# Time mixing's chunk recurrence: heads in pairs on diagonal corners of the array

## The chip, the core and the metric

One core of a Trainium2 chip. Its engines run side by side, each with its own list of instructions: TensorE (PE in the profile, its weight loads PEld) multiplies matrices into PSUM, VectorE (DVE) and ScalarE (ACT) work element by element, GpSimd (POOL) does a few small operations, and SyncE (SP) issues most transfers. The metric is the device time of one execution in microseconds; lower is better.

## The reference

A decoder block over 2048 tokens of 1024 channels. After a norm and one large projection, half of the mixing is RWKV-7 time mixing with 8 heads of 64 channels, half is differential attention with 4 heads; then an output projection and a gated MLP with a short convolution follow. The change lies in the time mixing, whose core is a recurrence over tokens with a 64 x 64 state per head:

```python
def step(state, inp):
    r_t, w_t, k_t, v_t, kk_t, a_t = inp
    sa = einsum('bhvk,bhk->bhv', state, -kk_t)
    state = (state * w_t[:, :, None, :]
             + sa[..., None] * (kk_t * a_t)[:, :, None, :]
             + v_t[..., None] * k_t[:, :, None, :])
    return state, einsum('bhvk,bhk->bhv', state, r_t)
```

All inputs and products of this part are float32.

## The kernel before

**Stages.** The input is projected in two halves of 1024 tokens (class `Proj`, tile `pp`, lines L99 to L101: each product is made of three, of high and low parts). The time mixing (class `Rwkv`) runs in 16 groups of 128 tokens; its stages are emitted in turns, a few after each block of the projection, later a few after each unit of the attention (class `Attn`: scores in a tile that is also called `sp`, L775 to L780; transposed weights `tp`, `at`; output `op`, L819). The output projection and the MLP come after both. Within an engine the order of instructions is fixed beforehand by a scheduler that goes through the program with modelled times; so products of the time mixing stand between projection matmuls or attention's, which fill TensorE while the recurrence waits for other engines.

**A group** is two chunks of 64 tokens (`NC` = 2). `prepare(g)` loads its rows, makes the decayed operands `AR` (64 columns against which the state is read for the recurrence, 64 for the output) and `BK` (b and k), the score products `se`, `so` of even and odd heads (L470), masks them into `M` (L474), sends the diagonal blocks through DRAM (`adr`, L478, then `ab`), transposes v into the lower half of `sav` (L490), and transposes `BK` into `bkt` (L497). `invert(g)` inverts 32 x 32 blocks on VectorE (L515, L517) and puts the result back into `M` by way of DRAM (`xdr`, L520, L523; `bda`, `bdx`, `x1t`); `join(g)` fills the block off the diagonal (`xp`, L545 to L554).

**`scan(g)`** goes through the two chunks. Channels lie on partitions, two heads (an even and an odd one) to a block of 128: index `hb` is the block, `e` the head in it. The state is kept as four 128 x 128 blocks whose corners off the diagonal stay zero. Per chunk:
- `rp` (L570, L573): for each block a product of the whole state block (128 rows, 64 columns of `AR`), then for each of the two heads a product of `M`'s lower half and `sav`'s lower half (key times value), added in PSUM; `rsb` is its copy by ScalarE (L575).
- `sp` (L578): eight products of the inverse in `M`'s upper half with `rsb`, all on partitions 0 to 63; copied into `sav`'s upper half (L579).
- `up` (L583): four 128 x 128 products of `bkt` and `sav`; VectorE adds the state's corners (L588) and multiplies by the decay (L591), a half of the partitions at a time.
- `yp` (L594, L597): per block one product of the state, then two of `sav`, 64 columns each; VectorE adds it to `ybv` (L600).

The previous group's `post` (norm and gate: tiles `mp`, `vs`, `gp`) is taken in between. The PSUM tiles of `scan`, `join` and `post` share the tag `rc` with two banks, those of `prepare` the tag `ra` with two, the projection has four (`mm`).

Of the kernel before, what the change touches and what calls it, by code (L numbers as in the profile page):

```python
# [34 lines left out]
def load_table(nc, cx, pool, eng, rows, name):  # L35
    """rows: list of DRAM APs [n, 128]; the result, once called, gives an SBUF tile [128, sum n] with the rows as
    columns."""
# [17 lines left out]
def rms_rstd(nc, cx, pool, src, n, eps, name, junk):  # L55
    """[128,1] = (mean(src^2) + eps)^-0.5 over the free axis; src is a list of APs."""
# [10 lines left out]
def norm_rows(nc, cx, pool, dst, src, gain, t):  # L67
    """dst = rms-normalised rows of src times gain; both SBUF [128, 1024], tokens x channels."""
# [9 lines left out]
def transpose_split(nc, cx, ps, xn, xh, xl, t, tag, bufs):  # L78
    """xn: SBUF [128, 1024] tokens x channels; writes tokens t*128.. of xh/xl, lists of [128, 8, GRP] tiles."""
# [16 lines left out]
def mm3(nc, out, lh, ll, rh, rl, n):  # L96
    """out = sum over kb of (lh+ll)^T (rh+rl) without ll*rl; callables give the operands of kb."""
    for kb in range(n):
        nc.tensor.matmul(out, lh(kb), rh(kb), start=(kb == 0), stop=False)  # L99
        nc.tensor.matmul(out, lh(kb), rl(kb), start=False, stop=False)  # L100
        nc.tensor.matmul(out, ll(kb), rh(kb), start=False, stop=(kb == n - 1))  # L101
# [24 lines left out]
class Proj:  # L126
    """Projections of x by w_in, one half of the tokens at a time."""
# [25 lines left out]
    def load(self, t, first=None):  # L153
        """128 tokens of normalised x, transposed and split; the second half's rows come from prepare()."""
# [22 lines left out]
    def prepare(self, t):  # L177
        """Normalises 128 tokens of the second half."""
# [14 lines left out]
    def pair(self, a, b, w=None):  # L193
        """Two blocks, the first tokens of both before the last."""
# [5 lines left out]
    def start(self, first):  # L200
        """Loads the first half and does its first two blocks."""
# [20 lines left out]
    def shift(self, cb, g, pp):  # L222
        """Token shift of an RWKV block."""
# [49 lines left out]
def rwkv_consts(tc, nc, cx, I):  # L273
# [46 lines left out]
    with tc.tile_pool(name="rkd", bufs=1, side="right") as pool:  # L320
        z = pool.tile([P, 4, P], F32, name="selz")
        nc.vector.memset(z, 1.0)
        # rows h of each 32-row block: 1 where 0 <= 128*hb + ch - 64*h < 64
# [23 lines left out]
    for i in range(2):  # L347
        s = c.tile([P, 4, P], F32, name=f"state{i}")
# [5 lines left out]
def rsqrt_bcast(nc, cx, pool, bank, op, val, i, nm):  # L354
    """bank: PSUM [128, 4, RG], whose first 8 columns hold a value for each token and head; it becomes
    op(value, val)^-0.5, channels x tokens."""
# [12 lines left out]
class Rwkv:  # L369
    """Time mixing, 128 tokens at a time, in four stages per group."""  # L370
# [12 lines left out]
    def prepare(self, g):  # L383
# [71 lines left out]
        tt(BK[:, :, :, 0, :], c4(b2), c4(ip), op=ALU.mult)  # L455
        tt(BK[:, :, :, 1, :], c4(kp), c4(ip), op=ALU.mult)
# [19 lines left out]
        for d in range(2):  # L476
            ds_ = slice(32 * d, 32 * d + 32)
            nc.sync.dma_start(adr[d].rearrange("b j i -> j b i"), M[ds_, :, :, ds_].rearrange("j c h i -> j (c h) i"))  # L478
# [10 lines left out]
        for q in range(2):  # L489
            nc.scalar.copy(sav[64:128, q].rearrange("p h x -> p (h x)"),  # L490
                           vt[64 * q:64 * q + 64].rearrange("p h x -> p (h x)"))
        bkt = T([P, NC, 512], "bkt", SB)
        for c in range(NC):
# [3 lines left out]
            nc.scalar.copy(bkt[:, c, :], bt.rearrange("p h x -> p (h x)"))  # L497

        self.live[g] = dict(AR=AR, M=M, sav=sav, bkt=bkt, ybv=ybv, pc=pc, sg=sg, X=X, ab=ab)
        yield  # L500

    def invert(self, g):
# [5 lines left out]
        for q in range(4):  # L508
            qs = slice(32 * q, 32 * q + 32)
            nc.sync.dma_start(cx.bda[qs, :, qs], mq[0:32, :, q, 32:64])  # L510
# [10 lines left out]
        for d in range(2):  # L521
            ds_ = slice(32 * d, 32 * d + 32)
            nc.sync.dma_start(M[ds_, :, :, ds_].rearrange("j c h i -> j (c h) i"),  # L523
                              xdr[d].rearrange("b m s i -> (m s) b i"))
# [10 lines left out]
    def join(self, g):  # L535
        """The blocks off the diagonal of the inverse."""
# [3 lines left out]
        mv = M.rearrange("p c h x -> p (c h) x")  # L540
# [13 lines left out]
        nc.scalar.copy(mv[0:32, :, 32:64], bank[0:32].rearrange("p t (q i) -> p (t q) i", q=4))  # L554
        yield

    def scan(self, g):
        """The state over the group's chunks, with the last group's post() in between."""
# [595 lines left out]
```

## Time and profile before

| | |
|---|---|
| median of 3 runs | 3289.52 us (3286.41 to 3295.87) |
| span of the profiled execution | 3295.9 us |
| TensorE busy | 3178.5 us, 96%, 16579 matmul instructions |
| VectorE, ScalarE, GpSimd busy | 1923.8, 1167.9, 332.6 us |
| bytes moved by DMA | 282.30 MB |

The profiled execution's own time stands at the upper end of the three; nothing of it lies around its span. Busy times of TensorE come from modelled ends of overlapping matmuls, so the distance from one start to the next says more than a duration.

### The profile page before, as it was taken

What the parts mean: (1) busy time and instruction counts of PE and PEld (TensorE: products, weight loads), DVE (VectorE), ACT (ScalarE), POOL (GpSimd) and SP (SyncE); (2) the same over time, 40 slices, a digit from 0 to 9 for tenths busy, and PEclk for the clock granted to TensorE, in tenths of its full rate; (3) what the DMA queues carried; (4) which work ended last, traced back from release to release, by engine and by line L of the source; (5) the groups of instructions that cost most, each with busy time, mean ns of one, the idle gap of its engine ahead of it and who ended that gap; (6) DMA issues with size and microseconds to landing.
All of it is one profiled execution on the core that took longest, in us unless ns stands there. A gap on an engine that the chain in (4) does not pass through costs nothing.

```text
span 3295.9 us, 44432 instructions
## 1 busy us (share of the span) xinstructions
PE 3178.5 (96%) x16579; PEld 2594.6 (79%) x16579; DVE 1923.8 (58%) x4898; ACT 1167.9 (35%) x2268; POOL 332.6 (10%) x441
## 2 busy tenths in 40 slices
PE   8999999999989989898999999999999999999997
PEld 6887777777777767677888888888888788888886
DVE  5246555455457868568655455555556655555556
ACT  4233322232225555467633422222223422222223
POOL 3001000010022232233200000000000000000002
PEclk9999999999878999899999999999999999999999
DMA  5355523234372252415244311111112411111112
GB/s 159 96 158 165 146 87 99 82 82 104 91 123 59 53 104 58 72 53 136 78 141 166 122 51 52 45 45 56 48 45 82 155 52 45 45 54 49 52 33 83
DMA packets 361177, 282.30 MB, mean 86 GB/s; under 512 B 95823, under 2 KB 307378, under 8 KB 360962
## 3 DMA queue, kind: packets, MB, share of 16 engines
q1 hardware_dynamic: 333874, 247.11, 25.9%
q0 software_dynamic: 24784, 28.16, 4.6%
q10 hardware_dynamic: 2304, 4.20, 0.4%
q8 instruction: 131, 2.15, 0.3%
q14 instruction: 84, 0.69, 0.1%
HBM read 204.72 MB, written 73.88 MB: 85 GB/s over the span
## 4 chain that ended last, share of the span: by engine, by line
PE 82%; DVE 4%; DMA 4%; issue 1%; ACT 1%; SPq 1%; POOL 0%; ACTq 0%; DVEq 0%; POOLq 0%
PE fp L99 10%; PE fp L101 9%; PE fp L100 9%; PE dn L100 5%; PE dn L99 5%; PE dn L101 5%; PE pp L99 4%; PE pp L100 4%; PE pp L101 4%; PE op L819 3%; PE po L99 2%; PE po L101 2%; PE sp L775 2%; PE po L100 2%; PE rp L573 2%; PE rp L570 2%
## 5 line engine op out<-in xcount | busy, mean ns | idle before, releaser
L1001 DVE TENSOR_TENSOR acc<-dn,acc 128x512 f32<-128x512 f32 x320 | 211.6, 688 | 224.3 <-PE dn L101 222.0
L99 PE MATMUL fp<-f1h,uh 128*128 128x512 f32 x704 | 275.8, 392 | 3.7 <-DVE fcarry L966 3.7
L100 PE MATMUL fp<-f1l,uh 128*128 128x512 f32 x704 | 275.2, 391 | 0.0
L101 PE MATMUL fp<-f1h,ul 128*128 128x512 f32 x704 | 275.1, 391 | 0.0
L100 PE MATMUL dn<-dl,gh 128*128 128x512 f32 x704 | 274.5, 390 | 0.0
L99 PE MATMUL fp<-f0h,uh 128*128 128x512 f32 x704 | 274.2, 389 | 0.0
L101 PE MATMUL fp<-f0h,ul 128*128 128x512 f32 x704 | 274.1, 389 | 0.0
L100 PE MATMUL fp<-f0l,uh 128*128 128x512 f32 x704 | 274.0, 389 | 0.0
L99 PE MATMUL dn<-dh,gh 128*128 128x512 f32 x704 | 271.7, 390 | 1.9 <-DVE acc L1001 1.9
L101 PE MATMUL dn<-dh,gl 128*128 128x512 f32 x704 | 263.4, 390 | 0.0
L780 DVE TENSOR_SCALAR_CACHE_REDUCE E<-sp 128x512 f32<-128x512 f32 (+3 forms) x320 | 188.4, 606 | 82.8 <-PE sp L778 45.7
L93 DVE TENSOR_TENSOR ul<-ur,uh 128x1024 fp32r<-128x1024 f32 x88 | 107.7, 1225 | 186.9 <-ACT uh L92 186.9
L962 DVE SCALAR_TENSOR_TENSOR u<-fp,cvA,u 128x511 f32<-128x511 f32 x176 | 131.4, 747 | 119.8 <-ACT u L960 119.8
L819 PE MATMUL op<-V,at 128*128 128x128 f32 x1088 | 163.6, 295 | 26.3 <-ACT at L815 25.3
L92 ACT CAST dh<-dr 128x1024 fp32r<-128x1024 f32 x44 | 44.4, 1047 | 386.6 <-PE dn L101 383.9
L819 PEld LDWEIGHTS op<-V,at 128*128 128x128 f32 x1088 | 146.1, 204 | 41.3 <-ACT at L815 32.7
L99 PE MATMUL pp<-x1h,wh 128*128 128x512 f32 x416 | 174.5, 419 | 0.0
L101 PE MATMUL pp<-x1h,wl 128*128 128x512 f32 x416 | 172.6, 415 | 0.0
L515 DVE TENSOR_TENSOR xtmp<-X,ab 128x60 f32<-128x60 f32 (+24 forms) x496 | 110.2, 222 | 105.9 <-DMA ab<-adr 76.2
L100 PE MATMUL pp<-x1l,wh 128*128 128x512 f32 x416 | 171.6, 412 | 0.0
L100 PE MATMUL pp<-x0l,wh 128*128 128x512 f32 x416 | 167.9, 404 | 0.0
L99 PE MATMUL pp<-x0h,wh 128*128 128x512 f32 x416 | 167.3, 403 | 0.1
(302 smaller groups left out, 7013.2 us busy)
## 6 DMA issues: line engine op xcount, KB each, us to landing
ur<-in_w_up SPq DMA_DIRECT2D x88, 512.0 KB
wr<-in_w_in SPq DMA_DIRECT2D x52, 512.0 KB
dr<-in_w_down SPq DMA_DIRECT2D x44, 512.0 KB
rw<-e SPq DMA_DIRECT2D x56, 256.0 KB
x<-in_x SPq DMA_DIRECT2D x16, 512.0 KB
qq<-e SPq DMA_DIRECT2D x64, 128.0 KB
kk<-e SPq DMA_DIRECT2D x64, 128.0 KB
ab<-adr SPq DMA_DIRECT2D x64, 128.0 KB
```

Source lines behind the costliest of these rows:

```text
L93: nc.vector.tensor_tensor(wl, wr, wh.bitcast(F32), op=ALU.subtract)
L99: nc.tensor.matmul(out, lh(kb), rh(kb), start=(kb == 0), stop=False)
L100: nc.tensor.matmul(out, lh(kb), rl(kb), start=False, stop=False)
L101: nc.tensor.matmul(out, ll(kb), rh(kb), start=False, stop=(kb == n - 1))
L515: tt(tv, X[:, 0:n, j:j + 1].broadcast_to([P, n, w]), ab[:, j:j + 1, j + 1:32].broadcast_to([P, n, w]), op=ALU.mult)
L570: nc.tensor.matmul(rp[0:64, 2 * hb:2 * hb + 2, :], AR[:, hb, c, 0, :], S[:, hb, :], start=True, stop=False)
L573: nc.tensor.matmul(rp[0:64, h, :], M[64:128, c, h, 0:64], sav[64:128, c, h, :], start=False, stop=(e == 1))
L775: nc.tensor.matmul(sp[:, 0:n], qa[:, c, qs], ka[:, c, 0:n], start=True, stop=False)
L780: nc.vector.tensor_scalar(e[ch * GRP // EW][:, eo:eo + n], sp[:, 0:n], -1.0, None, op0=ALU.mult, op1=ALU.min, accum_out=mx[:, ch:ch + 1])
L819: nc.tensor.matmul(op, at[:, q, :], v[:, q, :], start=(kb == 0), stop=(kb == qb))
L962: stt(u[:, 1:GRP], pp[:, 0:GRP - 1], w1(b), u[:, 1:GRP], op0=ALU.mult, op1=ALU.add)
L1001: nc.vector.tensor_tensor(acc[:, t, ds_], po, acc[:, t, ds_], op=ALU.add)
```

## The change

The two heads of a block are put on opposite corners: an even head on partitions 0 to 63, an odd one on 64 to 127, in every tile of the recurrence. For that, odd heads get b and k in exchanged places in `BK` (so `M`'s two halves are exchanged for them, and `sav`'s), and the transfers and copies that go by halves are split by `e`. The state keeps only its 64 columns per head. The product of key and value no longer stands in `rp`: `prepare` makes it once per group for both chunks (`wp`, copied to `kv` by ScalarE), and VectorE adds it to `rp`. In `scan` each form of product is issued for all eight heads in turn, even and odd alternating: `rp`, `sp`, the state's part of `yp`, `up`, then the rest of `yp`. The diff also drops docstrings; its core:

```diff
@@ rwkv_consts
-        s = c.tile([P, 4, P], F32, name=f"state{i}")
+        s = c.tile([P, 4, 64], F32, name=f"state{i}")
@@ prepare
-        tt(BK[:, :, :, 0, :], c4(b2), c4(ip), op=ALU.mult)
-        tt(BK[:, :, :, 1, :], c4(kp), c4(ip), op=ALU.mult)
+        for e in range(2):
+            rs = slice(64 * e, 64 * e + 64)
+            tt(BK[rs, :, :, e, :], c4(b2[rs]), c4(ip[rs]), op=ALU.mult)
+            tt(BK[rs, :, :, 1 - e, :], c4(kp[rs]), c4(ip[rs]), op=ALU.mult)
...
         for d in range(2):
-            ds_ = slice(32 * d, 32 * d + 32)
-            nc.sync.dma_start(adr[d].rearrange("b j i -> j b i"), M[ds_, :, :, ds_].rearrange("j c h i -> j (c h) i"))
+            for e in range(2):
+                r = 64 * e + 32 * d
+                nc.sync.dma_start(adr[d].rearrange("(b e) j i -> e j b i", e=2)[e],
+                                  M[r:r + 32, :, :, 32 * d:32 * d + 32].rearrange("j c (b e) i -> e j (c b) i", e=2)[e])
...
         for q in range(2):
-            nc.scalar.copy(sav[64:128, q].rearrange("p h x -> p (h x)"),
-                           vt[64 * q:64 * q + 64].rearrange("p h x -> p (h x)"))
+            for e in range(2):
+                nc.scalar.copy(sav[64 * (1 - e):64 * (1 - e) + 64, q].rearrange("p (b e) x -> e p b x", e=2)[e],
+                               vt[64 * q:64 * q + 64, :, 64 * e:64 * e + 64])
...
+        kv = T([P, NC, 4, 64], "kv", SB)
+        wp = U([P, NC, 4, 64], "wp")
+        for c in range(NC):
+            for hb in range(4):
+                for e in range(2):
+                    h, ks = 2 * hb + e, slice(64 * (1 - e), 64 * (1 - e) + 64)
+                    nc.tensor.matmul(wp[64 * e:64 * e + 64, c, hb, :], M[ks, c, h, 0:64], sav[ks, c, h, :],
+                                     start=True, stop=True)
+        nc.scalar.copy(kv, wp)
@@ invert
-            nc.sync.dma_start(cx.bda[qs, :, qs], mq[0:32, :, q, 32:64])
+            r = 64 * (q % 2)
+            nc.sync.dma_start(cx.bda[qs, :, qs], mq[r:r + 32, :, q, 32:64])
...
-            ds_ = slice(32 * d, 32 * d + 32)
-            nc.sync.dma_start(M[ds_, :, :, ds_].rearrange("j c h i -> j (c h) i"),
-                              xdr[d].rearrange("b m s i -> (m s) b i"))
+            for e in range(2):
+                r = 64 * e + 32 * d
+                nc.sync.dma_start(M[r:r + 32, :, :, 32 * d:32 * d + 32].rearrange("j c (b e) i -> e j (c b) i", e=2)[e],
+                                  xdr[d].rearrange("(b e) m s i -> e (m s) b i", e=2)[e])
@@ join
-        nc.scalar.copy(mv[0:32, :, 32:64], bank[0:32].rearrange("p t (q i) -> p (t q) i", q=4))
+        mv = M.rearrange("p c (b e) x -> e p (c b) x", e=2)
+        bv = bank[0:32].rearrange("p t (b e i) -> e p (t b) i", b=2, e=2)
+        for e in range(2):
+            nc.scalar.copy(mv[e][64 * e:64 * e + 32, :, 32:64], bv[e])
@@ scan
+        both = [(hb, e, 2 * hb + e, slice(64 * e, 64 * e + 64)) for hb in range(4) for e in range(2)]
...
+            rp = U([P, 4, 64], f"rp{c}")
+            for hb, e, h, rs in both:
+                nc.tensor.matmul(rp[rs, hb, :], AR[rs, hb, c, 0, :], S[rs, hb, :], start=True, stop=True)
+            rsb = kv[:, c]
+            tt(rsb, rp, rsb, op=ALU.add)
+            sp = U([P, 4, 64], f"sp{c}")
+            for hb, e, h, rs in both:
+                nc.tensor.matmul(sp[rs, hb, :], M[rs, c, h, 0:64], rsb[rs, hb, :], start=True, stop=True)
+            sv = sav[:, c].rearrange("p (b e) x -> e p b x", e=2)
             for e in range(2):
                 rs = slice(64 * e, 64 * e + 64)
+                nc.scalar.copy(sv[e][rs], sp[rs])
+            next(post, None)
             yp = U([P, 4, 64], f"yp{c}")
+            for hb, e, h, rs in both:
+                nc.tensor.matmul(yp[rs, hb, :], S[rs, hb, :], AR[rs, hb, c, 1, :], start=(hb == 0), stop=False)
+            up = U([P, 4, 64], f"up{c}")
+            for hb, e, h, rs in both:
+                nc.tensor.matmul(up[rs, hb, :], bkt[:, c, 64 * h:64 * h + 64], sav[:, c, h, :], start=True, stop=True)
+            st = T([P, 4, 64], "st")
+            tt(st, S, up, op=ALU.add)
+            tt(Sn, st, pc[:, :, c:c + 1].broadcast_to([P, 4, 64]), op=ALU.mult)
+            for hb, e, h, rs in both:
+                nc.tensor.matmul(yp[rs, hb, :], sav[:, c, h, :], M[:, c, h, 64:128], start=False, stop=(hb == 3))
```

The lines that `scan` loses are those of the kernel before, printed above.

## Rows read from the trace of the kernel before

**Rows 1.** The page: busy us by engine; the chain that ended last.

```profile
PE 3178.5 (96%) x16579; PEld 2594.6 (79%) x16579; DVE 1923.8 (58%) x4898; ACT 1167.9 (35%) x2268; POOL 332.6 (10%) x441
...
PE 82%; DVE 4%; DMA 4%; issue 1%; ACT 1%; SPq 1%; POOL 0%; ACTq 0%; DVEq 0%; POOLq 0%
```

**Rows 2.** Busy us by stretch; PEclk is the granted clock's mean.

```profile
280.00:960.00 680.00, 677.27 (x3968) 537.22 (x3968) 363.59 (x1039) 197.95 (x375) 63.17 (x62) 0.94 0.41 105
960.00:1440.00 480.00, 431.91 (x3024) 350.29 (x3023) 333.69 (x1224) 245.65 (x598) 122.35 (x162) 0.88 0.37 72
```

**Rows 3.** The chain of 960 to 1440 us by line.

```profile
by line: PE op L819 12.6%; PE sp L775 7.4%; DMA adr<-M 6.3%; PE tp L813 6.2%; PE sp L776 5.8%; PE rp L573 5.1%; PE rp L570 4.9%; DVE E L780 4.0%; PE sp L578 3.1%; PE yp L594 2.9%; DMA xdr<-X 2.7%; PE yp L597 2.6%; PE up L583 2.3%; issue 1.6
```

**Rows 4.** TensorE's waits, 960 to 1440 us: total, times, longest, us.

```profile
PE op L819 <- ACT at L815: 16.8, 8, 12.5
...
PE rp L570 <- DVE ybv L600: 7.4, 1, 7.4
```

**Rows 5.** Instructions on tile rp in the two stretches (ACT: the copies).

```profile
280.00:960.00 680.00, 64.30 (x456) 41.18 (x456) 11.00 (x19) 0.94 0.41 105
960.00:1440.00 480.00, 51.28 (x312) 31.43 (x312) 7.50 (x13) 0.88 0.37 72
```

**Rows 6.** TensorE's timeline around one rp block: start, duration in us.

```profile
917.84 0.40 PE L99 MATMUL pp<-x1h,wh 128*128 128x512 f32 x1
918.08 0.39 PE L100 MATMUL pp<-x1l,wh 128*128 128x512 f32 x1
918.40 0.43 PE L570 MATMUL rp<-state,AR 128*64 128x128 f32 x2
918.76 0.44 PE L573 MATMUL rp<-sav,M 64*64 64x64 f32 x4
919.14 0.43 PE L570 MATMUL rp<-state,AR 128*64 128x128 f32 x2
...
921.34 0.27 PE L425 MATMUL n<-ones2c,t_a 128*128 128x2 f32 x1
```

**Rows 7.** TensorE's timeline around one sp block.

```profile
304.98 1.14 PE L578 MATMUL sp<-rsb,M 64*64 64x64 f32 x16
306.05 0.50 PE L100 MATMUL pp<-x0l,wh 128*128 128x512 f32 x1
```

**Rows 8.** TensorE's timeline, one up block and yp block.

```profile
910.06 1.06 PE L583 MATMUL up<-sav,bkt 128*128 128x128 f32 x8
910.96 0.33 PE L594 MATMUL yp<-AR,state 128*128 128x64 f32 x2
911.22 0.34 PE L597 MATMUL yp<-M,sav 128*64 128x64 f32 x4
911.49 0.43 PE L594 MATMUL yp<-AR,state 128*128 128x64 f32 x2
...
913.38 0.38 PE L418 MATMUL za<-alx,lora 65*128 65x128 f32 x1
```

**Rows 9.** TensorE's timeline, score products of even and odd heads.

```profile
219.18 0.27 PE L470 MATMUL se<-AR,BK 64*128 64x128 f32 x1
219.19 0.27 PE L470 MATMUL so<-AR,BK 64*128 64x128 f32 x1
219.29 0.27 PE L470 MATMUL se<-AR,BK 64*128 64x128 f32 x1
```

**Rows 10.** Groups by line and form: busy us, mean ns; idle before.

```profile
L588 DVE TENSOR_TENSOR st<-state,up 64x256 f32<-64x256 f32 x64 | 26.6, 416 | 7.4 <-PE up L583 6.1
...
L575 ACT COPY rsb<-rp 64x512 f32<-64x512 f32 x32 | 18.5, 578 | 52.9 <-PE rp L573 52.5
...
L600 DVE TENSOR_TENSOR ybv<-yp,ybv 128x256 f32<-128x256 f32 x32 | 13.5, 422 | 2.5 <-PE yp L597 2.1
...
L455 DVE TENSOR_TENSOR BK<-t_e,t_d 128x512 f32<-128x512 f32 x16 | 12.1, 758 | 0.2
```

**Rows 11.** The issues of one transfer: ns min/median/max.

```profile
L478 SPq DMA_DIRECT2D adr<-M x32: 303/480/700, 231.0 to 1308.5; - x32
```

More of the change, by code (lines that the diff above doesn't have):

```diff
@@ L497, in prepare @@
             nc.scalar.copy(bkt[:, c, :], bt.rearrange("p h x -> p (h x)"))
-        self.live[g] = dict(AR=AR, M=M, sav=sav, bkt=bkt, ybv=ybv, pc=pc, sg=sg, X=X, ab=ab)
+        kv = T([P, NC, 4, 64], "kv", SB)
[7 more added lines that the diff above has]
+        nc.scalar.copy(kv, wp)
+        self.live[g] = dict(AR=AR, M=M, sav=sav, bkt=bkt, ybv=ybv, pc=pc, sg=sg, X=X, ab=ab, kv=kv)
         yield
@@ L539, in join @@
         M, x1t = L["M"], L["x1t"]
-        mv = M.rearrange("p c h x -> p (c h) x")
         bank = UC([P, 4, P], "xp")
@@ L563, in scan @@
         L = self.live[g]
-        AR, M, sav, bkt, ybv, pc = (L[n] for n in ("AR", "M", "sav", "bkt", "ybv", "pc"))
+        AR, M, sav, bkt, ybv, pc, kv = (L[n] for n in ("AR", "M", "sav", "bkt", "ybv", "pc", "kv"))
+        both = [(hb, e, 2 * hb + e, slice(64 * e, 64 * e + 64)) for hb in range(4) for e in range(2)]
         for c in range(NC):
@@ L567, in scan @@
             cx.scur = 1 - cx.scur
-            rp = U([P, 8, 64], f"rp{c}")
-            for hb in range(4):
-                nc.tensor.matmul(rp[0:64, 2 * hb:2 * hb + 2, :], AR[:, hb, c, 0, :], S[:, hb, :], start=True, stop=False)
-                for e in range(2):
-                    h = 2 * hb + e
-                    nc.tensor.matmul(rp[0:64, h, :], M[64:128, c, h, 0:64], sav[64:128, c, h, :], start=False, stop=(e == 1))
-            rsb = T([P, 8, 64], "rsb")
-            nc.scalar.copy(rsb[0:64], rp[0:64])
@@ L576, in scan @@
-            sp = U([P, 8, 64], f"sp{c}")
-            for h in range(8):
-                nc.tensor.matmul(sp[0:64, h, :], M[0:64, c, h, 0:64], rsb[0:64, h, :], start=True, stop=True)
-            nc.scalar.copy(sav[0:64, c], sp[0:64])
-            next(post, None)
-            up = U([P, 4, P], f"up{c}")
-            for hb in range(4):
-                nc.tensor.matmul(up[:, hb, :], bkt[:, c, hb * P:(hb + 1) * P], sav[:, c, 2 * hb:2 * hb + 2, :],
-                                 start=True, stop=True)
@@ L585, in scan @@
-            st = T([P, 4, 64], "st")
+            rp = U([P, 4, 64], f"rp{c}")
[7 more added lines that the diff above has]
+            sv = sav[:, c].rearrange("p (b e) x -> e p b x", e=2)
@@ L586, in scan @@
             for e in range(2):
                 rs = slice(64 * e, 64 * e + 64)
-                tt(st[rs], S[rs, :, rs], up[rs, :, rs], op=ALU.add)
-            for e in range(2):
-                rs = slice(64 * e, 64 * e + 64)
-                tt(Sn[rs, :, rs], st[rs], pc[rs, :, c:c + 1].broadcast_to([64, 4, 64]), op=ALU.mult)
+                nc.scalar.copy(sv[e][rs], sp[rs])
+            next(post, None)
             yp = U([P, 4, 64], f"yp{c}")
-            for hb in range(4):
-                nc.tensor.matmul(yp[:, hb, :], S[:, hb, :], AR[:, hb, c, 1, :], start=True, stop=False)
-                for e in range(2):
-                    h = 2 * hb + e
-                    nc.tensor.matmul(yp[64 * e:64 * e + 64, hb, :], sav[:, c, h, :], M[:, c, h, 64:128],
-                                     start=False, stop=True)
+            for hb, e, h, rs in both:
+                nc.tensor.matmul(yp[rs, hb, :], S[rs, hb, :], AR[rs, hb, c, 1, :], start=(hb == 0), stop=False)
@@ L602, in scan @@
             yield
-        del L["AR"], L["M"], L["sav"], L["bkt"]
+        del L["AR"], L["M"], L["sav"], L["bkt"], L["kv"]
     def post(self, g):
```

## The prediction

> **What bounds the kernel.** I began with the busy shares and the chain that ended last [rows 1]: TensorE is busy 96% of the span and holds 82% of the chain; no other engine (PEld is its own weight loads) reaches 60%. The change touches only the time-mixing class, so the question is when that runs and what bounds it then. The busy time by stretch, cut at 960 us where the projections end and attention begins, shows two regimes [rows 2]. From 280 to 960 us TensorE is busy 677 of 680 us; all other engines have room. From 960 to 1440 us it is busy 432 of 480 us, and the chain there also names transfers and VectorE: adr<-M 6.3%, xdr<-X 2.7%, E L780 4.0% [rows 3]. TensorE's list of waits for that stretch has few and short ones, which name ScalarE, VectorE and landings [rows 4]. By tile, the scan copies rsb 19 times in the first stretch and 13 times in the second [rows 5]: that is where its 32 chunks lie. The reader should take from this that a microsecond of TensorE time saved in the first stretch is a microsecond, and in the second less. How much less is a choice: of the terms that the chain's row names [rows 3] TensorE's come to 53% of the stretch and others' to 15%; half of the unnamed 32% added, I credit 0.7. The busy share, 0.9, is the most it can be.
>
> **A chunk's price on TensorE before.** I count from the first start of a block to the start of what comes next, since the durations of matmuls overlap. Every float32 product is two instructions, each with a weight load.
> The block rp [rows 6] starts at 918.40 and the next work at 921.34: 2.94 us for 24 instructions. It changes form eight times. The last projection matmul before it starts 0.32 us ahead of it where its neighbours stand 0.24 apart, so coming from one form into another costs about 0.09 us more.
> The block sp [rows 7], 16 instructions on one corner, takes 306.05 - 304.98 = 1.07, and with the same entry 1.16.
> up [rows 8] takes 910.96 - 910.06 = 0.90, at the filler's own form; yp takes 913.38 - 910.96 = 2.42, with seven changes of form inside.
> Sum: 2.94 + 0.09 + 1.16 + 0.90 + 2.42 = 7.51 us a chunk, 240 us for 32.
>
> **Price per instruction.** Four instructions of 64 rows and 64 columns on one corner take 919.14 - 918.76 = 0.38 us including the change to the next form [rows 6]; sixteen take 1.07 [rows 7]. So one more costs (1.07 - 0.38) / 12 = 0.058 us.
>
> **Do two halves of the array run at once?** Two rows of the trace bear on it. The score products se and so lie on the upper and lower 64 rows: they start in pairs 0.01 us apart, and the next pair follows after 0.11 us [rows 9], which is what one alone of that width takes (up: 0.90 / 8 = 0.11). And yp's two products for an even and an odd head (four instructions), on the left and right 64 columns, take 911.49 - 911.22 = 0.27 us to the next form [rows 8], where four on one corner take 0.38: two instructions at 0.058 less, as if each half did its two side by side. No row shows corners on the diagonal, which differ in rows and columns both, nor a long series of such pairs of 64 columns. The bounds: 0.058 us for a pair (fully side by side) and 0.116 (one after the other). I take 0.058, since both kinds of half do it.
>
> The Trainium skill (TensorE: Matmul & The Clock Gate, Part 3, The mechanism) says that a weight load overlaps matmuls in flight only when the row group differs. By that up and the second part of yp, which use all rows and half the columns, would stay serial (the sum of rival 2); yp's 0.27 us [rows 8] speaks against it, and the sum below goes by the row.
>
> **A chunk's price after.** A paired block of 16 (eight on each corner) costs 0.38 + 4 x 0.058 = 0.61, with entry 0.70.
> - rp is now only the state's products: 0.70. sp: 0.70. The state's part of yp: 0.70.
> - up and the second part of yp have one form and follow each other: 16 instructions on each half, 1.07 + 0.09 = 1.16.
> - The new key-value products, wp, once a group: 32 instructions, 1.16, so 0.58 a chunk.
> Sum 3.84; saved 7.51 - 3.84 = 3.67 us a chunk. If pairs run one after the other: three blocks at 1.16, 32 instructions at 1.07 + 16 x 0.058 + 0.09 = 2.09, wp 1.05: 6.62, saved 0.89.
> In time: 19 x 3.67 = 70 us in the first stretch, 13 x 3.67 x 0.7 = 33 in the second: 103.
>
> **What is added elsewhere**, per group of two chunks. VectorE: the BK products go from two to four instructions of the same length per partition, +2 x 0.76; the sum into rsb replaces ScalarE's copy, at yp's final sum's 0.42, twice; the state needs four instructions where it had eight, -4 x 0.42 [rows 10]. That is +0.7 us a group, 11 us over 1160 us in which it is busy 697; hidden behind TensorE except where VectorE is on the chain, 1 us. The choice of engine for rsb has a price of its own: sp now waits behind VectorE's queue (the inversion's short steps, attention's reductions), where it waited behind ScalarE's. In the first stretch projection matmuls cover it; without that cover it is one queued instruction, up to about 0.7 us a chunk (BK's 0.76 is the longest of the class).
> ScalarE: -2 copies of 0.578 (rsb), +1 of that size (kv), and five copies become ten of half the length; no row has that length, so 0.29 to 0.58 each: between -0.6 and +2.3 us a group. It is busy 444 of 1160 us: nothing.
> SP's queue: adr and M<-xdr go from two transfers to four each, so four more issues a group at 0.48 us [rows 11], with the same bytes. adr stands ahead of ab, for which the inversion waits, and ahead of bda; M's stand ahead of bdx and x1t, which join waits for. In the first stretch join's work is ahead of need. In the second adr<-M is 6.3% of the chain, 30 us. Bounds: half of it back (twice as many partitions serve one block) to 7 groups x 4 x 0.48 = 13 lost; I take 3 lost.
> The state's part of yp is moved ahead of up: up, the new state and the next rp stand 0.7 us later. Between up at 910.06 and the next rp at 918.40 lie 8.3 us of other work [rows 6, 8], so nothing; without that cover 0.7 x 32 = 22.
>
> **Clock.** The granted clock has a mean of 0.94 and 0.88 in the two stretches [rows 2]. As it is 2.4 or 1.2 GHz, 0.94 is 12% of 680 us at 1.2, which loses 41 us of TensorE's work. Whether the shorter sparse blocks keep it up no row tells: 0 to 41 back; I take 8, since half-used array remains.
>
> Sum: 103 - 1 - 3 + 8 = 107. The profiled execution spans 3295.9 us; 3295.9 - 107 = 3189. It is the slowest of the three runs, 6.4 above their median, so 3183 for a median.
>
> **Rivals.**
> 1. Corners take turns (a pair at 0.116). For it: no such pair in the trace. Against it: [rows 9]. Saved 19 x 0.89 + 13 x 0.89 x 0.7 = 25, and nothing else changes much: 3265. The Trainium skill (same page, Wait — 56ns, not 53.3ns?) tells of about 62 ns a matmul when the sequencer decodes by software, which would make a pair 0.124 and give this case; sp's 0.058 a matmul is already below it.
> 2. Only the diagonal corners pair; the two halves of columns don't: up and yp's second part at 2.09 instead of 1.16. Saved 3.67 - 0.93 = 2.74 a chunk: 52 + 25 = 77, time 3183 + 26 = 3209.
> 3. Slower, by one wait. The tag rc has two banks, which rp, sp, yp, up and the outputs' tiles share. yp now keeps one from its first product until the sum behind its last, across up, so up must find the other free. If TensorE then stands at up until VectorE has freed it, work behind it in its queue stands too. The trace has one such wait, rp for the sum of yp, 7.4 us [rows 4]. At every chunk that would be 32 x 7.4 = 237: 3183 + 237 = 3420. It decides from 107 / 32 = 3.3 us a chunk. Against it: one wait in 32 so far, and the tile that held the bank (mp) is freed by one VectorE instruction.
> 4. The change shortens the blocks but the order of the rest, which is worked out from modelled times, turns worse, or waits for adr and x1t take up the gain: about 3290. Against it: 19 chunks lie in a stretch without waits.
>
> **How the numbers follow.** Forecast 0.65 (its own range 3150 to 3216: at one end all of the second stretch's 48 us credited and 27 of the clock's 41 back, 14 and 19 more than assumed; at the other nothing of the second stretch, 33 less). Rival 1 0.13, rival 2 0.10, rival 3 0.07, rival 4 0.05. The range of 3150 to 3266 takes in the forecast and rivals 1 and 2, and leaves out rivals 3 and 4 and some of the forecast's tails. A measurement of this kernel tells about 0.3%, 10 us, from no change: faster 0.65 + 0.13 + 0.10 = 0.88, same 0.05, slower 0.07.
>
> **What would show it.** In the profile after: rp, sp and the first part of yp at 0.6 us a block of 16, with starts in pairs 0.01 apart (0.058 from pair to pair); at 1.07, rival 1. up and yp's second part in 1.07 together, or 2.0 (rival 2). Matmul instructions of the class by 32 x 24 = 768 more, and TensorE's busy time down all the same. Waits of TensorE before up that name VectorE: rival 3. The scan's last product about 90 us earlier. The prediction fails if the first stretch doesn't shorten by some 65 us, or if the attention after it gives the gain back in waits.

## The result, and the profile after

The changed kernel takes 3186.73 us in the median of four runs (3179.55 to 3194.09), against 3292.69 for the kernel before on the same chip (four runs, 3286.41 to 3309.11): a ratio of 0.9677, 95% interval 0.9643 to 0.971. The profiled execution spans 3188.7 us. The forecast was 3183, and 107 us less for the span of the profiled execution; it is 107.2 less. The total is right, but two of its terms were wrong in opposite directions; most of both is the same work, counted in another stretch than it was reckoned for.

The page of the changed kernel, busy times and the chain, as [rows 1]:

```profile
PE 3042.6 (95%) x17347; PEld 2499.7 (78%) x17347; DVE 1920.9 (60%) x4898; ACT 1170.6 (37%) x2332; POOL 329.1 (10%) x441
...
PE 77%; DVE 6%; DMA 4%; ACT 1%; SPq 1%; issue 1%; POOL 0%; DVEq 0%; ACTq 0%; POOLq 0%
```

TensorE has 768 more matmul instructions, as counted, and 135.9 us less busy time. Only 107.2 of that reach the span: busy time and span lie 146.1 us apart now, where they lay 117.4 apart. In the chain TensorE has lost five points of share and VectorE has gained two. The engines that were to be hidden did not change (VectorE 1920.9 for 1923.8 us).

The stretches of the changed kernel, with the columns of [rows 2]; the last is that of [rows 2], the first ends where the projections now end:

```profile
280.00:842.00 562.00, 552.16 (x4081) 443.46 (x4081) 334.38 (x943) 185.54 (x376) 47.51 (x45) 0.98 0.44 119
842.00:960.00 118.00, 85.42 (x796) 70.04 (x794) 79.80 (x316) 56.51 (x149) 38.37 (x50) 0.80 0.60 106
960.00:1440.00 480.00, 425.59 (x3468) 354.23 (x3469) 366.71 (x1288) 282.73 (x692) 132.18 (x177) 0.89 0.40 82
```

The last projection product starts at 840.3 us and not at 942.7: 102 us of the gain are there already. The 118 us behind it are the emptiest stretch of this part: TensorE is busy 72% of them, at a mean granted clock of 0.80. In the kernel before, the 118 us behind its last projection product (942.7 to 1061) are busy 86%, at a clock of 0.73: the low clock there is not new. Later stages keep their length (output projection 190.5 and 190.0 us, MLP 1474.1 and 1475.7).

TensorE's timeline around the blocks rp, sp with yp, and up with yp, for [rows 6 to 8]:

```profile
318.31 0.68 PE L589 MATMUL rp<-state,AR 64*64 64x64 f32 x16
318.92 1.05 PE L425 MATMUL n<-ones2c,t_a 128*128 128x2 f32 x8
...
307.65 0.68 PE L594 MATMUL sp<-kv,M 64*64 64x64 f32 x16
308.16 0.63 PE L602 MATMUL yp<-AR,state 64*64 64x64 f32 x16
308.72 0.50 PE L99 MATMUL pp<-x0h,wh 128*128 128x512 f32 x1
...
312.87 0.27 PE L610 MATMUL yp<-M,sav 128*64 128x64 f32 x1
312.88 0.27 PE L605 MATMUL up<-sav,bkt 128*64 128x64 f32 x1
312.98 0.22 PE L610 MATMUL yp<-M,sav 128*64 128x64 f32 x1
312.99 0.62 PE L605 MATMUL up<-sav,bkt 128*64 128x64 f32 x14
313.44 0.22 PE L610 MATMUL yp<-M,sav 128*64 128x64 f32 x1
313.44 0.22 PE L605 MATMUL up<-sav,bkt 128*64 128x64 f32 x1
313.50 0.57 PE L610 MATMUL yp<-M,sav 128*64 128x64 f32 x13
314.00 0.50 PE L101 MATMUL pp<-x0h,wl 128*128 128x512 f32 x1
```

Sixteen instructions (eight products) on corners take 318.92 - 318.31 = 0.61 us (rp), 0.51 (sp) and 0.56 (yp's part of the state): diagonal corners work side by side. The 32 instructions of up and yp's second part take 314.00 - 312.87 = 1.13: so do halves of columns that share all their rows. For this last, the prediction read a sentence of the Trainium skill (TensorE: Matmul & The Clock Gate, Part 3, The mechanism: a weight load overlaps matmuls in flight only when the row group differs) to mean that the two halves go one after the other; the measurement decides against that reading.

### The profile page after: what moved, and what is told of

Read it like the earlier page. It is cut to its first block, busy times and chain, and to the rows that moved or that the text cites. A ratio compares the mean times of both kernels' runs of the same rounds, so it can differ in the third digit from the quotient of the medians.

```text
span 3188.7 us, 46110 instructions
## 1 busy us (share of the span) xinstructions
PE 3042.6 (95%) x17347; PEld 2499.7 (78%) x17347; DVE 1920.9 (60%) x4898; ACT 1170.6 (37%) x2332; POOL 329.1 (10%) x441
## 4 chain that ended last, share of the span: by engine, by line
PE 77%; DVE 6%; DMA 4%; ACT 1%; SPq 1%; issue 1%; POOL 0%; DVEq 0%; ACTq 0%; POOLq 0%
PE fp L99 10%; PE fp L101 10%; PE fp L100 10%; PE dn L100 5%; PE dn L99 5%; PE dn L101 5%; PE pp L99 4%; PE pp L101 4%; PE pp L100 4%; PE op L831 3%; PE po L99 2%; PE po L101 2%; PE po L100 2%; PE sp L787 2%; PE sp L788 1%
## 5 line engine op out<-in xcount | busy, mean ns | idle before, releaser
L801 ACT ACTIVATE E<-E,asc 128x1024 f32<-128x1024 f32 (+7 forms) x160 | 153.7, 963 | 54.9 <-DVE asc L797 54.6
```

The costliest lines, as they stand in the source:

```text
L801: nc.scalar.activation(e[i][:, 0:n], e[i][:, 0:n], AF.Exp, bias=nm, scale=-1.0, accum_out=z)
```

## The experiments

Each kernel alters the changed kernel, unless it says otherwise. Ratios are to the kernel before, on the same chip. "Scan" is TensorE's time in rp, sp, yp, up and wp, each instruction counted to the start of the next, over the whole execution: 255.1 us before, 129.8 after. Where TensorE waits behind such an instruction, the wait is in the figure; with each instruction counted at most to its own end it is 255.1 and 125.1.

**The changed kernel once more** (no edit).

> The changed kernel once more, beside the three that follow, as their anchor: its median within 0.3% of the 3186.7 us of its first runs, by every theory.

3189.34 us (3180.49 to 3197.12), ratio 0.9678 [0.9655, 0.97]. The ratio repeats to 0.0001; single runs of one kernel lie up to 17 us apart.

**Grouping alone, in the kernel before.** Heads stay where they were; rp does its four state products and then its eight key-value products, and yp likewise.

```diff
             for hb in range(4):
-                nc.tensor.matmul(rp[0:64, 2 * hb:2 * hb + 2, :], AR[:, hb, c, 0, :], S[:, hb, :], start=True, stop=False)
-                for e in range(2):
-                    ...
+                nc.tensor.matmul(rp[0:64, 2 * hb:2 * hb + 2, :], AR[:, hb, c, 0, :], S[:, hb, :], start=(hb == 0), stop=False)
+            for h in range(8):
+                nc.tensor.matmul(rp[0:64, h, :], M[64:128, c, h, 0:64], sav[64:128, c, h, :], start=False, stop=(h == 7))
...
-                nc.tensor.matmul(yp[:, hb, :], S[:, hb, :], AR[:, hb, c, 1, :], start=True, stop=False)
+                nc.tensor.matmul(yp[:, hb, :], S[:, hb, :], AR[:, hb, c, 1, :], start=(hb == 0), stop=False)
+            for hb in range(4):
```

> The kernel before with one part of the change alone: in rp the four products of the state come first and the eight of key and value after them, in yp the four of the state and then the eight of sav; heads stay where they were. Theory (changes of form are dear even without corners): rp goes from 2.94 to about 2.1 us, yp from 2.42 to about 1.5, 1.75 us a chunk, 56 us of TensorE's time, of which 40 to 56 show: 3239 to 3255 us. Rival (nearly all of the gain comes from two corners at work at once): within 15 us of the kernel before, 3278 to 3295.

3244.98 us (3225.03 to 3251.13), ratio 0.9853 [0.9822, 0.9885]: 46 us of the change's gain of about 106 come from grouping products of one form, without any pairing of corners; this is what the theory expected. The scan falls from 255.1 to 201.7 us (rp from 110.4 to 79.4, yp from 77.7 to 51.1). The remaining 60 us or so belong to the pairing of corners and to the key-value products taken out of rp.

**yp's forms mixed again.** up comes first, then for each block the state's pair and sav's pair.

```diff
-            for hb, e, h, rs in both:
-                nc.tensor.matmul(yp[rs, hb, :], S[rs, hb, :], AR[rs, hb, c, 1, :], start=(hb == 0), stop=False)
             up = U([P, 4, 64], f"up{c}")
...
+            for b in range(4):
+                for hb, e, h, rs in both[2 * b:2 * b + 2]:
+                    nc.tensor.matmul(yp[rs, hb, :], S[rs, hb, :], AR[rs, hb, c, 1, :], start=(hb == 0), stop=False)
+                for hb, e, h, rs in both[2 * b:2 * b + 2]:
+                    nc.tensor.matmul(yp[rs, hb, :], sav[:, c, h, :], M[:, c, h, 64:128], start=False, stop=(hb == 3))
```

> The two parts of yp alternate again, block by block, after up; the pairs stay side by side. Theory (a change of form costs about 0.1 us each way, beside the pairing): 8 pieces of four instructions at 0.27 us instead of 0.61 + 0.47: about 1 us a chunk, 32 us, of which 22 to 32 show: 3209 to 3219 us. Rival (form changes are hidden or cheap, pairing is all of it): no more than 10 us slower.

3224.01 us (3215.39 to 3232.71), ratio 0.9781 [0.9761, 0.9801]: 35 us above the two medians of the changed kernel (3187 and 3189), a little more than the theory's range. TensorE's timeline of one yp:

```profile
316.65 0.33 PE L609 MATMUL yp<-AR,state 64*64 64x64 f32 x4
316.91 0.34 PE L611 MATMUL yp<-M,sav 128*64 128x64 f32 x4
317.17 0.33 PE L609 MATMUL yp<-AR,state 64*64 64x64 f32 x4
317.43 0.34 PE L611 MATMUL yp<-M,sav 128*64 128x64 f32 x4
```

Two pairs of instructions (four, of one even and one odd head) take 0.26 us to the next form. In a grouped block two pairs take two steps of 0.058, 0.116; so a change of form costs about 0.145 us here, and yp has seven where it had none: 1.0 us a chunk, 32 us in all. The scan has grown by 28.0, to 157.8.

**Evens, then odds.** The same products, but all even heads' before all odd heads' in each block.

```diff
-        both = [(hb, e, 2 * hb + e, slice(64 * e, 64 * e + 64)) for hb in range(4) for e in range(2)]
+        both = [(hb, e, 2 * hb + e, slice(64 * e, 64 * e + 64)) for e in range(2) for hb in range(4)]
```

> Same products, but each form is issued for the four even heads and then for the four odd ones, so that neighbours in the list stand on the same corner. Theory (the gain is two corners or halves at work at once): a block of 16 goes from 0.6 to about 1.07 us, up with the second part of yp from 1.07 to 2.0, wp from 1.07 to 2.0; 3.84 to 6.62 us a chunk, 2.8 x 32 = 89 us of TensorE's time, of which 60 to 89 show: 3247 to 3276 us. Rival (the gain is fewer changes of form and less work, the order of even and odd doesn't matter): within 10 us of the changed kernel, 3177 to 3197.

3218.51 us (3207.73 to 3222.74), ratio 0.9762 [0.9741, 0.9783]: about 30 us slower than the change. This lies between the two expectations, and neither mechanism is right as it was put. TensorE's timeline around sp and the state's part of yp:

```profile
311.04 0.40 PE L99 MATMUL pp<-x0h,wh 128*128 128x512 f32 x1
311.37 0.79 PE L594 MATMUL sp<-kv,M 64*64 64x64 f32 x13
311.94 0.27 PE L602 MATMUL yp<-AR,state 64*64 64x64 f32 x1
311.99 0.22 PE L594 MATMUL sp<-kv,M 64*64 64x64 f32 x1
312.05 0.22 PE L602 MATMUL yp<-AR,state 64*64 64x64 f32 x1
...
312.16 0.74 PE L602 MATMUL yp<-AR,state 64*64 64x64 f32 x13
312.83 0.50 PE L100 MATMUL pp<-x0l,wh 128*128 128x512 f32 x1
```

In TensorE's list all 16 instructions of sp stand ahead of yp's. Yet yp's first starts at 311.94, when three of sp's are still to start: instructions on one corner pass instructions listed earlier that wait for the other. The 32 instructions take 312.83 - 311.37 = 1.46 us: longer than the 308.72 - 307.65 = 1.07 of the alternating order, and well under the 2 x 1.07 that one corner after the other would take [rows 7]. So TensorE finds part of the pairing by itself, and the alternating order is worth what it doesn't find: the scan takes 179.0 us instead of 129.8. Only about 30 of these 49 us show in the time: in the profiled execution, span and busy time lie 116.3 us apart here and 146.1 in the changed kernel, so part of what the pairing saves is lost again in waits.

**The sum of rp and kv on TensorE.** An identity's corner times kv is added to rp in PSUM, and ScalarE copies rp, as in the kernel before.

```diff
+            for e in range(2):
+                rs = slice(64 * e, 64 * e + 64)
+                nc.tensor.matmul(rp[rs], cx.ident[rs, rs], kv[rs, c], start=False, stop=True)
-            tt(rsb, rp, rsb, op=ALU.add)
+            nc.scalar.copy(rsb, rp)
```

> The key-value product is added to rp by TensorE (a product of the identity's corner and kv, 256 columns, one for each half) and rsb is ScalarE's copy of the sum, so that sp no longer waits behind VectorE's queue. Theory (the wait of 13.5 us of sp for VectorE's sum, which stood behind the inversion's first step, is a cost of the changed kernel): the two products cost about 0.25 us a chunk, 8 us in all, and 13 us of waits go: 3177 to 3187 us, with no wait of sp for VectorE. Rival (that wait stands in front of the same late transfer either way, and something else waits for it): 3190 to 3200 us.

3200.39 us (3192.79 to 3206.65), ratio 0.9711 [0.9691, 0.9731]. Two instructions per corner of 64 x 256 lengthen rp by 20 us over all (24.7 to 45.1): the timeline has rp's sixteen from 314.34 and the four from 314.86 to 315.39. The theory had reckoned 8 us for them. The wait of sp for VectorE, shown below, is gone (longest stall of TensorE where the attention begins 4.4 us), and the time is longer all the same. But in this kernel adr leaves at 839.1 to 840.7 us and ab follows it after 1.8 us: the late transfer behind that wait did not occur here. So this run prices the two products; it does not test what the wait costs.

**The sum on GpSimd.** ScalarE copies rp, GpSimd adds kv.

```diff
-            tt(rsb, rp, rsb, op=ALU.add)
+            rs0 = T([P, 4, 64], "st")
+            nc.scalar.copy(rs0, rp)
+            nc.gpsimd.tensor_tensor(rsb, rs0, rsb, op=ALU.add)
```

> The changed kernel with the sum of rp and kv made by GpSimd from ScalarE's copy of rp, so that neither VectorE's queue nor added TensorE work stands before sp. Theory (the one wait of 13.5 us of sp for VectorE costs its length, and the longer way, about 1 us a chunk, is covered): 3172 to 3182 us. Rival (the wait only stands in front of the same late transfers, and the way by two engines is longer): 3187 to 3205.

3189.84 us (3183.92 to 3192.07), ratio 0.9699 [0.9681, 0.9717], against 0.9677: no gain. To see why, first the stall in the changed kernel. Its list of TensorE's waits, 842 to 1530 us (total, times, longest), as [rows 4]:

```profile
PE op L831 <- ACT at L827: 27.1, 26, 4.9
PE sp L594 <- DVE kv L591: 13.5, 1, 13.5
PE vp L750 <- DMA vtl<-vT: 11.3, 2, 8.6
```

and its timeline of all engines, where the attention begins (in brackets the idle time before, and what ended it):

```profile
843.47 3.63 SPq L481 DMA_DIRECT2D adr<-M  x4
...
844.56 1.23 POOL L743 DMA_DIRECT2D ka<-kk  x2
...
860.37 1.93 SPq L485 DMA_DIRECT2D ab<-adr  x4
...
872.50 0.19 DVE L530 TENSOR_TENSOR xtmp<-X,ab 128x31 f32<-128x31 f32 x1 [14.72 <-DMA alx<-rw]
...
873.53 1.12 PE L594 MATMUL sp<-kv,M 64*64 64x64 f32 x16 [13.55 <-DVE kv L591]
```

TensorE stands at sp for VectorE's sum. But VectorE itself has idled 14.72 us: the sum stands in its list behind an inversion's first step, which reads ab (the bracket names the transfer that landed last by the profile). ab was issued 14.2 us after the start of adr's last issue, while GpSimd issued the attention's first loads (most of them from 841 on), and the step that reads ab followed 12.1 us after ab's first issue. For the other groups the distance from adr to ab is 1.8 to 4.2 us, but for two later ones, with 6.8 and 8.1. With the sum on GpSimd, this is what TensorE waited for:

```profile
PE op L833 <- ACT at L829: 15.5, 18, 4.6
PE tp L827 <- DVE E L814: 14.1, 5, 11.9
```

The 13.5 us at sp are gone, and 11.9 stand at the attention's transposes, which wait for VectorE behind the same late ab (issued at 868.12, 16.4 us after adr). The engine of the sum was not what mattered for this stall.

**The attention's first loads held back** until ab of that group has landed (a small copy on GpSimd reads ab; the loads of 17 units go behind it).

```diff
+            nc.gpsimd.tensor_copy(cx.warm, rw.live[9]["ab"][:, 0, 0:1])
+            late = nc.cur_bb.bb.instructions[-1]
...
+                        with tc.issue_after(late):
+                            next(units)
```

> The changed kernel with attention's first loads on GpSimd's queue held back until the ninth group's diagonal blocks (adr, ab) have landed, by a one-column GpSimd copy that reads ab and that the loads stand behind. Theory (adr of that group leaves 2.5 us after those loads and lands 14 us late behind them; VectorE's first inversion step waits for it, and TensorE behind VectorE for 13.5 us; kv inside the scan was faster in part because there adr left 8 us ahead of them): adr to ab takes 2 to 4 us, no wait of 10 us or more at the start of attention, 3170 to 3180 us. Rival (the wait at that place is one of many and comes back elsewhere): 3184 to 3200.

3177.81 us (3174.43 to 3187.54), ratio 0.9666 [0.9644, 0.9688]. The two transfers and the inversion's first step, in its timeline:

```profile
843.34 1.90 SPq L482 DMA_DIRECT2D adr<-M  x4
848.06 1.72 SPq L486 DMA_DIRECT2D ab<-adr  x4
...
853.41 0.19 DVE L531 TENSOR_TENSOR xtmp<-X,ab 128x31 f32<-128x31 f32 x1 [6.20 <-DMA ab<-adr]
```

adr lands in time, ab follows after 3.3 us and its reader 5.4 us after ab's first issue, and no stall over 4.7 us is left at this place. That the burst of loads delayed the two transfers here is shown. The time did not follow beyond doubt: the intervals of the two ratios overlap almost wholly, and in this kernel the ab of a later group followed its adr only after 14.1 us. Against the kernel before on the same chip this one gains 112 us where the change gained 106: for one removed stall of 13.5 us that is 6 us, within the noise.

**The state's part of yp after up**, where the kernel before had it.

```diff
-            yp = U([P, 4, 64], f"yp{c}")
-            for hb, e, h, rs in both:
-                nc.tensor.matmul(yp[rs, hb, :], S[rs, hb, :], AR[rs, hb, c, 1, :], start=(hb == 0), stop=False)
             up = U([P, 4, 64], f"up{c}")
...
+            yp = U([P, 4, 64], f"yp{c}")
+            for hb, e, h, rs in both:
+                nc.tensor.matmul(yp[rs, hb, :], S[rs, hb, :], AR[rs, hb, c, 1, :], start=(hb == 0), stop=False)
```

> The state's part of yp stands after up again, directly before the second part; nothing else changes. Theory (the place of that block costs nothing but two more changes of form a chunk, 0.1 to 0.15 us each): 6 to 10 us slower than the changed kernel, 3193 to 3199. Rival (the block before up delays the recurrence by 0.5 us a chunk): as much as 16 us faster, 3170 to 3185.

3182.9 us (3177.41 to 3185.57), ratio 0.9673 [0.9654, 0.9692]: the same as the change within the noise. The loss of 6 to 10 us that the theory expected did not come; the number lies in the rival's range, but the run can't tell a gain of a few us from none. Its place costs nothing that can be measured.

**The key-value products back in the scan**, in a block of their own ahead of rp, once a chunk, with a ScalarE copy each and a tile in rc.

```diff
+            wp = U([P, 4, 64], f"wp{c}")
+            for hb, e, h, rs in both:
+                ks = slice(64 * (1 - e), 64 * (1 - e) + 64)
+                nc.tensor.matmul(wp[rs, hb, :], M[ks, c, h, 0:64], sav[ks, c, h, :], start=True, stop=True)
+            rsb = T([P, 4, 64], "kv", SB)
+            nc.scalar.copy(rsb, wp)
             rp = U([P, 4, 64], f"rp{c}")
...
-            rsb = kv[:, c]
```

> The key-value product is made per chunk inside the scan again, on the same corners, in a PSUM tile of its own, copied by ScalarE and added by VectorE as before; the number of products is unchanged. Theory (once per group or per chunk is the same for TensorE, only one entry of 0.1 us a chunk more): 3 us, and up to 10 for a third tile in a row on two PSUM banks: 3187 to 3200. Rival (taking it out of the scan is a main part of the gain): 3210 us or more.

3160.15 us (3155.28 to 3167.79), ratio 0.9608 [0.9586, 0.963]: some 25 us faster than the change (131 us below the kernel before on the same chip, where the change lies 106 below), the fastest kernel of this study, and outside both expectations. TensorE has slightly more to do (busy 3049.4 for 3042.6; the scan's 148.4 us, with 31.8 for wp instead of 18.0, is in good part waits behind its instructions, one of 6.6 us behind wp, and without them 129.5 for 125.1). But its busy time and its span of 3154.8 lie 105.4 us apart instead of 146.1. The gain is in waits: the projections end 8 us later, and from there to the end of the attention's products it takes 641.5 us for 682.3, of which 38 are idle time of TensorE. Its list of TensorE's waits there begins

```profile
PE op L826 <- ACT at L822: 15.1, 18, 3.9
PE vp L745 <- DMA vtl<-vT: 10.7, 2, 6.4
PE sp L782 <- DMA qa<-qq: 4.2, 1, 4.2
```

**The key-value products once a group, in join.** The loops are those of the change; only the stage differs, and the tile takes one of the banks of rc.

```diff
 (prepare)
-        wp = U([P, NC, 4, 64], "wp")
-        ...
-        nc.scalar.copy(kv, wp)
 (join)
+        wp = UC([P, NC, 4, 64], "wp")
+        ...
+        nc.scalar.copy(kv, wp)
```

> The key-value product is made once per group, as in the changed kernel, but in join, directly before the scan, in the scan's PSUM banks. Theory A (what the product costs in prepare is its place: banks and ScalarE's copies ahead of the next group): as fast as kv inside the scan, 3150 to 3170 us. Theory B (kv inside the scan is faster by where the transfers fall, not by the place of the product): 3175 to 3200 us, with a late adr at the start of attention, or as fast as 3165 without one.

3162.74 us (3159.04 to 3166.77), ratio 0.9616 [0.9599, 0.9633]: like the kernel with the products in the scan, with one block a group, and as theory A has it. So the number of these blocks isn't what matters; and in this kernel ab followed 11.8 us after adr at the attention's start, so the late transfer alone isn't either.

**Both moves together**: the products in the scan, and the state's part of yp after up (the two edits above).

> kv inside the scan, and the state's part of yp after up. Theory (the place of that block is free, two more changes of form cost 6 to 10 us): 3160 to 3172 us where adr at the start of attention is early. Rival (the order gives the recurrence 0.5 us a chunk): 3145 to 3155.

3184.07 us (3179.61 to 3193.78), ratio 0.9676 [0.9657, 0.9695]. This is outside both expectations, and the theory's condition, an early adr, did not hold. An edit that alone cost nothing takes back the 25 us that the other alone had won. TensorE's waits in this part have a new entry, again behind a late adr (16.0 us to ab):

```profile
PE rp L585 <- ACT kv L582: 18.9, 2, 18.8
```

**The key-value products in prepare, but in a bank of rc.**

```diff
-        wp = U([P, NC, 4, 64], "wp")
+        wp = UC([P, NC, 4, 64], "wp")
```

> The changed kernel, with one thing altered: the tile wp of the key-value products, still made in prepare, takes one of the recurrence's two PSUM banks (tag rc) and not one of prepare's two (tag ra). The two kernels that moved wp out of prepare were some 25 us faster than the change (3160 and 3163) and had both moved it into rc as well. Theory bank: what costs is that wp holds a bank of ra until ScalarE has copied it, so that prepare's next products wait; then this kernel takes 3150 to 3172. Theory place: what costs is that the products and their copy stand in prepare, ahead of the inversion, whatever the bank; then 3178 to 3196, as the change itself (3187). A time above 3200 would say that rc has no bank to spare while a scan runs, and that TensorE waits there for ScalarE's copy.

3231.57 us (3215.29 to 3245.76), ratio 0.9808 [0.9771, 0.9846]: 45 us slower than the change by one letter. Neither theory had this; the third case gave a time above 3200, but by a wait that the list of waits doesn't show. What the profile shows is order. TensorE's wp between 280 and 842 us, of this kernel:

```profile
L509 PE MATMUL wp<-sav,M 64*64 64x64 f32 x224 | 10.3, 224 | 0.0
```

Seven groups are prepared there (224 of 512 instructions, 32 a group) where the change has eight (256), and the attention's first units stand there instead. The groups of instructions on the attention's output, of this kernel and of the change (count; ns min/median/max; first and last start):

```profile
L831 PE MATMUL op<-V,at x1088: 272/275/582, 824.1 to 1579.5; 128*128 128x128 f32 x182
```

```profile
L831 PE MATMUL op<-V,at x1088: 270/275/583, 880.8 to 1522.8; 128*128 128x128 f32 x182
```

It begins 57 us earlier and ends 57 us later. The likely reading is that the recurrence, a group behind, fills TensorE less well beside the attention: it is busy 412 of the 480 us from 960 to 1440, for 426, and the granted clock of 960 to 1440 us has a mean of 0.83 for 0.89. Whether it was rc's banks that put it back isn't shown. The gain of the kernels with these products in the scan and in join doesn't come from the bank alone.

## Why the prediction was right, step by step

**Price of paired blocks: right.** 0.61, 0.51 and 0.56 us for 0.61 to 0.70, 1.13 for 1.16; rivals 1 and 2, corners or halves of columns in turn, are refuted by the rows above. The scan's total fell by 125.3 us (by 130.0 without the waits in it) where 32 x 3.67 = 117 were reckoned.

**First stretch: 70 reckoned, 102 measured.** 19 chunks were multiplied by 3.67. Cut at the last projection product (942.7 and 840.3 us), the scan's own time there fell by 76. Another 6.5 came from projection matmuls, whose time fell from 625.5 to 619.0. The remaining 20 is other work, net of idle time, which rose from 0.5 to 9.8 us (from 280 us on). Part of the 102 was not saved but moved out: the projections are through earlier, and only 17 chunks have begun beside them instead of 18 (rp), 16 instead of 18 have got to sp, and 304 instructions on se and so stand there instead of 320, 164 on xp instead of 180. At the prices of the kernel before, what is missing there is worth about 25 us, half of it in the scan's 76 (an estimate from these counts). The 77 that stay are what this stretch's two terms, 70 and 8 for the clock, come to together. The step that failed took the split of the chunks from the kernel before and held it fixed; its 19 is also one too many, from a cut at 960 us, where the projections end at 942.7.

**Attention's stretch: 33 reckoned, 6 measured.** From the end of the projections to that of the attention's products it is 688.2 us before and 682.3 after. The scan's time there fell by 49, close to 13 x 3.67 = 48, though one to two chunks more stand there; but TensorE's idle time there rose from 68.1 to 89.8 us, and the work moved out of the first stretch came in. The factor of 0.7 for the second stretch was too high: with some 20 us set aside for the moved work at its price after (an estimate), 26 of the 49 reached the time, about half. This is rival 4 in small, whose mechanism (waits for adr, a worse order) took about 22 us here. The chain of 960 to 1440 us names xdr<-X at 3.3%, E at 4.9% and the attention's own lines; the long wait for adr now stands ahead of 960.

**How the total still came out.** The misses of 32 and 27 are mostly the same work, which left one stretch and entered the other. That 107.2 came out for 107 is luck beyond that: 26 for 33 in the attention's stretch is offset by about 5 us that the moved work itself saved (25 at the old price, 20 at the new, both estimates) and by the losses of 1 and 3 us, which no run shows by themselves.

**Sum on VectorE: cost in the wrong place.** It was priced at up to 0.7 us a chunk where cover is missing, "one queued instruction". The actual wait was one of 13.5 us, for a whole idle VectorE queue behind a late transfer. With the sum on GpSimd the same delay reaches TensorE by another way (11.9 us at the transposes); with the sum on TensorE the late transfer did not occur.

**adr's transfers: 3 lost was the wrong kind of number.** More issues cost little in the first stretch. But where the attention's loads begin, ab came 14.2 us after adr, as it did in the kernel before (15.0, and the stall of 7.4 in [rows 4]). In the kernel before, the sum of L600, for which TensorE waits there, stands in VectorE's list just behind the inversion's first step:

```profile
975.93 1.72 SPq L481 DMA_DIRECT2D ab<-adr  x4
979.92 0.19 DVE L515 TENSOR_TENSOR xtmp<-X,ab 128x31 f32<-128x31 f32 x1 [8.77 <-DMA ab<-adr]
980.27 0.42 DVE L600 TENSOR_TENSOR ybv<-yp,ybv 128x256 f32<-128x256 f32 x1
```

So the late transfer was there already; in the changed kernel TensorE waits for it at another place, and longer (13.5 for 7.4).

**Clock: 8 reckoned, more came back.** The projection matmuls alone give 6.5. By the prediction's own arithmetic, a mean granted clock of 0.95 from 280 to 942.7 us loses 33 us of TensorE's work and 0.98 from 280 to 840.3 us loses 11, so about 22 came back (an estimate; part of it lies in the scan's 76). The term was too small, and no row shows the reason given for taking 8. From 960 to 1440 us the mean is 0.89 for 0.88.

**The rest.** VectorE's and ScalarE's busy times, up by 11 and a few us at most, came out at -2.9 and +2.7. The products into BK take 0.803 (b) and 0.688 us (k) each, for 0.76 reckoned; the sum into rsb takes 0.420, as reckoned. Moving yp's state part cost nothing, as the experiment on it shows. Rival 3, TensorE at up for a bank of rc, has no entry in the list of waits of the changed kernel. One more tile in rc, in prepare, did cost 45 us, by another way.

**Where the gain comes from.** About 46 of 106 us come from grouping by form, and the alternation of corners is worth about 30 in the changed kernel. The remaining 30 are put down to what TensorE pairs by itself and to the key-value products' block; no run separates these. The parts don't add exactly, as every version also has another order.

**What stays open.** Why the key-value products in prepare cost some 20 to 25 us against the scan or join. It isn't their count (scan and join agree), nor the late adr alone (join has it), nor their bank alone (prepare with rc is worse). That leaves the stage, or simply the order that the scheduler makes of it: an edit that is worth nothing alone took 25 us from a better order. The runs cannot separate these two.

## What to carry to other kernels

Small products on a tiled array are worth grouping by form first (0.145 us a change of form here, 46 of the 106 us without any other edit), and then alternating between corners, since TensorE by itself finds only part of the pairs. Price such a gain by stretch: where TensorE has no waits nearly all of it comes back, while beside work that waits for others about half of it returned as idle time here, and the split of the work between the stretches moves. Where a scheduler fixes the order, take differences of up to some 25 us between near variants as possibly a property of that order, and try the moved piece at two or three places (here scan or join instead of prepare gave 3160 and 3163 us, 4% under the kernel before).

## What the runs showed of the hardware that was not expected

- Products of different corners don't keep the list's order: yp's first start at 311.94 lies ahead of three starts of sp, listed before it. The Trainium skill says of matmuls that they stay in program order (TensorE: Matmul & The Clock Gate, Part 3, The mechanism), and also that tiles operate independently (TensorEngine Tiling (Array Packing), Key Properties); this row agrees with the second.
- A change between products on 64 x 64 corners and on 128 x 64 halves costs about 0.145 us (two pairs at 0.26 us instead of 0.116).
- The transfers of adr (four of 32 KB; two of 64 KB where M is not split) were followed by their reader ab after 12 to 16 us in eight of the fourteen kernels, where the attention begins and GpSimd issues its loads, and after 3.3 us with these loads held back. Later groups show such a delay too, now and then (15.5 us in the kernel before, 18.8 with the products in join).
